# Two products of each row pair first, and low parts by transfers, in a two-layer Fourier and attention encoder

## The chip, the cores and the metric

The kernel runs on one core of one Trainium2 chip. The metric is the device time of one execution in microseconds, the median of several. The core's engines run side by side, each with its own queue in program order: TensorE (PE, matrix products, with weight loads shown apart as PEld), VectorE (DVE), ScalarE (ACT), GpSimd (POOL) and SyncE (SP), which issues transfers. Products go into PSUM, which has eight banks here; everything else works in SBUF.

## The reference

Two layers on x, 512 positions by 1024 channels, float32:

```python
for l in range(DEPTH):
    h = rmsnorm(x, norm1[l])
    p = h @ w_in[l]                       # u (512) | q (8 x 64) | k (2 x 64) | v (2 x 64)
    y_f = fourier_mix(u, w_fourier[l], b_fourier[l])     # Re FFT over positions and channels, then @ w_f + b_f
    y_a = windowed_gqa(rope(rmsnorm(q)), rope(rmsnorm(k)), v, sink[l])   # |i - j| <= 128, learned sink
    x = x + concat(rmsnorm(y_f), rmsnorm(y_a)) @ w_o[l]
    h = rmsnorm(x, norm2[l])
    up = dwconv_centred(h @ w_up[l], conv_w[l], conv_b[l])   # 2 x 2816 columns, 3 taps along positions
    gate, val = up[..., :D_FF], up[..., D_FF:]
    x = x + (silu(gate) * val) @ w_down[l]
```

## The kernel before, in words

Everything is kept transposed: x is eight tiles of 128 channels by 512 positions (`x[0]` to `x[7]`). A matrix product in nearly full precision is done as three: each operand is split into a high part (a copy in the format float32r, written by ACT) and a low part (source minus high part, written by DVE), and `mm3` (L114) issues high by high, low by high and high by low. `split` (L98) does this for activations and `wsplit` (L132) for weights, into rotating buffers `whi` and `wlo`, five each. A `wsplit` reads a raw weight tile, `wraw` (three buffers of 128 x 1024), that `wload` (L127) brings through SP's queue.

**The feed-forward half of a layer** goes through the 22 blocks of 128 hidden channels in three groups of 8, 8 and 6 (`GROUPS`, L35; `kp` is half of that: 4, 4, 3). A group has two stages.

*Up projection* (L756 to L780). For each hidden block and each of gate and value: load 512 KB of `w_up`, two `wsplit`s, 24 matmuls into one PSUM bank; then DVE scales by the norm (`u`), ACT starts the convolution (`y`), DVE adds its other two taps. Silu and the product of gate and value give one block's activations. Two blocks make a pair, an upper and a lower one, from which `seven_gu` (L382) forms the right-hand operands of seven products: B11 from the upper block alone, the others (T1 to T4, B21, B22) from sums and differences of both blocks' halves. Their high and low parts go into parts of buffers that attention doesn't need at that time (`pieces`, L375; the names slab, pT and m4 in the profile).

*Down projection, the product stage* (L782 to L798). The output's 1024 channels are four pairs of tiles (`mp`), the 512 positions two halves, a group's hidden blocks two halves as well: a 2 x 2 by 2 x 2 block product that is done with seven products rather than eight. `seven_w` (L401) loads two tiles a and b of `w_down` (for the pair's two output tiles; the first half of each are the upper hidden blocks, the second half the lower ones: a11, a12, a21, a22) and yields, in this order, a weight, the bank part and the operand:

| product | weight | bank part | operand |
|---|---|---|---|
| 1 | a11 | X | B11 |
| 2 | s1 = a21 + a22 | Y | T1 |
| 3 | s2 = a11 - s1 | X | T2 |
| 4 | a12 | Z | B21 |
| 5 | s3 = a11 - a21 | X | T3 |
| 6 | s4 = a12 + s2 | Y | B22 |
| 7 | a22 | X | T4 |

The sums are DVE's, in buffers `tF` (six). X and Y share a PSUM bank and go on accumulating; after each product DVE adds the present content to a quarter of x. All seven of a row pair are done before the next pair's first. The banks are taken in turn from six (`FFN_BANKS`, L34). In layer 1's last group each quarter is sent out when its last term is in.

**Work done ahead for layer 1.** During layer 0's feed-forward half, `presplit` (L149) is a generator with 44 jobs, one for each tile of layer 1's weights, in the order qkv (16), u (8), f (4), o (16). A job loads a tile (`praw`, two buffers), folds it if it is u or f (DVE, into `tA`), splits it into two `tA` buffers (six in all) and stores both parts to DRAM (`kept`); the stores are called one job later. `fetch` (L193) loads the parts in layer 1. The loop calls `next(ahead)` once for every up projection and once at the first row pair of every product stage (L774, L784).

**What sets the order.** The program text gives each instruction a priority. A planner then simulates the program and puts on each engine's queue, at each moment, the earliest instruction in the text whose inputs and buffers are ready; a later one can so be put ahead of an earlier one that still waits. Buffers of one name are given out in the order of the text. On the chip each queue runs in the order so found. `tc.issue_after(ins)` ties the instructions of a block that are on the engine of `ins` behind `ins` in that queue, without waiting for it to finish.

Of the kernel before, what the change touches and what calls it, by code (L numbers as in the profile page):

```python
# [16 lines left out]
P = 128  # L17
D = 1024
S = 512
L = 2  # L20
# [17 lines left out]
def encoder_kernel(tc, t):  # L38
# [92 lines left out]

    def wsplit(raw, eng=None, hi_eng=None):  # L132
        hi = wp.tile([P, 512], F32R, tag="whi", name=nm("whi"), bufs=5)
        lo = wp.tile([P, 512], F32R, tag="wlo", name=nm("wlo"), bufs=5)
        n = raw.shape[-1]
        if hi_eng is None:
            act(hi[:, :n], raw)
        else:
            hi_eng.tensor_copy(hi[:, :n], raw)
        tt(lo[:, :n], raw, f(hi)[:, :n], ALU.subtract, eng)  # L140
        return hi, lo
# [7 lines left out]
    def presplit(l):  # L149

        late = []

        def keep(key, src):
            n = src.shape[-1]
            two = [temp(n, "tA", F32R) for _ in range(2)]
            split(two[0], two[1], src)
            kept[key] = [dp.tile([P, n], F32, tag=f"{key}{s}", name=nm("kept")) for s in range(2)]
            store()
            late.append(lambda: [nc.sync.dma_start(o, f(z)) for o, z in zip(kept[key], two)])

        def store():
            while late:
                late.pop()()

        def load(src):
            raw = temp(512, "praw")[:, :src.shape[-1]]
            nc.sync.dma_start(raw, src)
            return raw

        jobs = []  # L170
        for grp in (1, 0):
            for k in range(KT):
                c = (k % 2) * 384
                jobs.append((f"qkv{grp}{k}", lambda g=grp, k=k, c=c: load(t["w_qkv"][l, g, k // 2, :, c:c + 384])))
        for k in range(KT):
            jobs.append((f"u{k}", lambda k=k: load(t["w_in"][l, k * P:(k + 1) * P, 0:FW])))
        for j in range(NF):
            jobs.append((f"f{j}", lambda j=j: load_wf(l, j, temp(512, "praw"))))
        for half in range(2):
            for m in range(KT):  # L180
                jobs.append((f"o{half}{m}", lambda h=half, m=m: load(t["w_o"][l, h, :, m * 512:(m + 1) * 512])))
        got = jobs[0][1]()
        for n, (key, _) in enumerate(jobs):
            raw = got
            if n + 1 < len(jobs):
                got = jobs[n + 1][1]()
            keep(key, fold_wu(raw) if key[0] == "u" else fold_wf(raw) if key[0] == "f" else raw)
            yield
        store()
        while True:  # L190
            yield
# [181 lines left out]
    LANDED = {3: (0, 0), 4: (1, 1), 5: (0, 1), 6: (1, 0)}  # L373
# [27 lines left out]
    def seven_w(l, m, f0, kp):  # L401

        n = kp * P
        a, b = [wload(t["w_down"][l, m + i, :, f0 * P:f0 * P + 2 * n], 2 * n) for i in range(2)]
        a11, a12, a21, a22 = a[:, :n], a[:, n:], b[:, :n], b[:, n:]
        yield "X", wsplit(a11), "B11", 0, 0
        s1 = temp(n, "tF")
        tt(s1, a21, a22, ALU.add)
        yield "Y", wsplit(s1), "T1", 1, 1
        s2 = temp(n, "tF")  # L410
        tt(s2, a11, s1, ALU.subtract)
        yield "X", wsplit(s2), "T2", 0, 1
        yield "Z", wsplit(a12), "B21", 0, 0
        s3 = temp(n, "tF")
        tt(s3, a11, a21, ALU.subtract)
        yield "X", wsplit(s3), "T3", 1, 1
        s4 = temp(n, "tF")
        tt(s4, a12, s2, ALU.add)
        yield "Y", wsplit(s4), "B22", 0, 1
        yield "X", wsplit(a22), "T4", 1, 0  # L420
# [4 lines left out]
    for l in range(L):  # L425
# [326 lines left out]
        for f0, nf in GROUPS:  # L752
# [3 lines left out]
            for n in range(nf):  # L756
                fi = f0 + n // 2 + kp * (n % 2)
                ys_ = []
                for z in range(2):
# [10 lines left out]
                    act(y, u, AF.Identity, scale=cw[:, l, 1, m:m + 1], bias=cb[:, l, m:m + 1])  # L770
# [3 lines left out]
                    next(ahead)  # L774
# [6 lines left out]
            nxt = []  # L781
            for mp in range(KT // 2):  # L782
                if mp == 0:
                    next(ahead)  # L784
                xy, zz = [psum(FFN_BANKS[(nps[0] + i) % len(FFN_BANKS)]) for i in (1, 2)]
                nps[0] += 2
                bank = dict(X=xy[:, :256], Y=xy[:, 256:], Z=zz[:, :256])
                for i, (b, w, g, r, c) in enumerate(seven_w(l, 2 * mp, f0, kp)):
                    m, q0 = 2 * mp + r, 256 * c
                    for k in range(kp):  # L790
                        mm3(bank[b], [z[:, k * P:(k + 1) * P] for z in w], gu[k][g], k == 0 and i in (0, 3), k == kp - 1,
                            skip_group_check=True)
                    tt(x[m][:, q0:q0 + 256], x[m][:, q0:q0 + 256], bank[b], ALU.add)
                    if l == L - 1 and f0 + nf == FT and i in LANDED:
                        m, q0 = 2 * mp + LANDED[i][0], 256 * LANDED[i][1]
                        nc.sync.dma_start(t["out"][m, :, q0:q0 + 256], x[m][:, q0:q0 + 256])
                if l < L - 1 and f0 + nf == FT:
# [90 lines left out]
```

## Time and profile before

| | us |
|---|---|
| median of 3 runs | 1156.58 (1156.01 to 1157.02) |
| the profiled execution | 1156.34 |
| its span, first to last instruction | 1154.5 |
| PE busy | 1052.4 (91%) |
| DVE busy | 903.7 (78%) |
| ACT busy | 561.6 (49%) |
| POOL busy | 63.2 (5%) |

The profile is one execution. Lines such as L93 or L120 are lines of helpers (`tt`, `mm3`), so that instructions are told apart by the tiles that they write and read: `wlo<-wraw,whi` is a low part of a weight, `x<-x,ps` an addition of a product to x, `m<-tF,m`, `pT<-tF,pT` and `slab<-tF,slab` low parts of activations. An entry in square brackets is idle time of the engine ahead of the instruction, and what ended it. The granted clock (PEclk) is that of TensorE, as a share of full speed. Durations of neighbouring DVE or PE instructions overlap a little, so that their rate is read from their starts.

### The profile page before, as it was taken

How to read it: one execution, taken by the hardware profiler on the slowest of the kernel's cores; microseconds unless marked ns; L12 is line 12 of the kernel's file. 1: busy time of each engine (PE TensorE's matmuls, PEld its weight loads, DVE VectorE, ACT ScalarE, POOL GpSimd, SP SyncE). 2: the span in 40 equal slices, each digit the busy share in tenths (PEclk: the TensorE clock that was granted, in tenths of full speed). 3: DMA queues.
4: the chain of work that ended last, by engine and by line, in shares of the span. 5: the costliest groups of instructions: out<-in, count | busy, mean ns of one | idle time of the engine just before them, and what ended most of it. 6: DMA issues, size and time to landing. Idle time of an engine off the chain costs nothing.

```text
span 1154.5 us, 16570 instructions
## 1 busy us (share of the span) xinstructions
PE 1052.4 (91%) x5866; PEld 913.0 (79%) x5866; DVE 903.7 (78%) x1841; ACT 561.6 (49%) x1055; POOL 63.2 (5%) x142
## 2 busy tenths in 40 slices
PE   8999998993699996999789999999979999799977
PEld 8977786882688886988679977888869888698867
DVE  7967759888877878778785877378988688886876
ACT  5269636565334543344442596246543454334532
POOL 0015200001000000000000044000000000000000
PEclk9999999997799998999899999999989999899989
DMA  8231387887133221332146622423313422133213
GB/s 274 82 110 30 110 273 252 291 286 268 55 110 110 92 73 55 110 110 78 41 137 207 195 74 74 128 92 91 100 46 93 127 91 92 54 95 113 91 43 100
DMA packets 61559, 140.18 MB, mean 121 GB/s; under 512 B 6818, under 2 KB 22178, under 8 KB 61476
## 3 DMA queue, kind: packets, MB, share of 16 engines
q1 hardware_dynamic: 61476, 139.12, 38.5%
q8 instruction: 46, 0.75, 0.3%
q14 instruction: 37, 0.30, 0.1%
HBM read 116.02 MB, written 23.07 MB: 120 GB/s over the span
## 4 chain that ended last, share of the span: by engine, by line
PE 68%; DVE 16%; DMA 9%; ACT 4%; issue 2%; POOL 0%; SPq 0%; DVEq 0%; ACTq 0%; POOLq 0%
PE ps L120 20%; PE ps L121 20%; PE ps L122 20%; DVE tF L93 5%; DMA wraw<-in_w_down_dram 4%; DVE wlo L93 4%; PE ps L118 3%; DMA praw<-in_w_o_dram 2%; DVE x L93 2%; DVE tF L96 1%; DMA praw<-in_w_qkv_dram 1%; PE ps L595 1%; ACT tA L90 1%; DVE tA L93 1%; PE ps L588 1%
## 5 line engine op out<-in xcount | busy, mean ns | idle before, releaser
L120 PE MATMUL ps<-act,whi 128*128 128x512 f32 x768 | 299.2, 390 | 3.1 <-ACT whi L90 1.4
L122 PE MATMUL ps<-act,whi 128*128 128x512 f32 x768 | 298.5, 390 | 0.6 <-DVE act L96 0.5
L121 PE MATMUL ps<-act,wlo 128*128 128x512 f32 x768 | 298.4, 390 | 0.0
L90 ACT ACTIVATE whi<-wraw 128x512 fp32r<-128x512 f32 (+1 forms) x272 | 166.6, 616 | 220.3 <-PE ps L122 211.2
L93 DVE TENSOR_TENSOR wlo<-wraw,whi 128x512 fp32r<-128x512 f32 (+1 forms) x280 | 186.1, 669 | 37.9 <-ACT whi L90 35.9
L120 PEld LDWEIGHTS ps<-act,whi 128*128 128x128 f32 x768 | 144.2, 188 | 34.6 <-ACT act L90 2.1
L122 PEld LDWEIGHTS ps<-act,whi 128*128 128x128 f32 x768 | 144.2, 188 | 30.8 <-DVE act L96 1.4
L121 PEld LDWEIGHTS ps<-act,wlo 128*128 128x128 f32 x768 | 144.2, 188 | 29.6 <-DVE wlo L93 0.3
L96 DVE SCALAR_TENSOR_TENSOR tF<-tF,pb,tF 128x511 f32<-128x511 f32 x176 | 130.1, 747 | 13.5 <-ACT tF L90 11.4
L120 PE MATMUL ps<-slab,whi 128*128 128x256 f32 (+2 forms) x272 | 90.2, 336 | 33.5 <-ACT whi L90 27.7
L93 DVE TENSOR_TENSOR x<-x,ps 128x256 f32<-128x256 f32 (+1 forms) x184 | 81.0, 441 | 46.9 <-PE ps L122 42.1
L121 PE MATMUL ps<-slab,wlo 128*128 128x256 f32 (+2 forms) x272 | 88.6, 326 | 27.6 <-DVE wlo L93 27.4
L93 DVE TENSOR_TENSOR tF<-ps,rb 128x512 f32<-128x512 f32 x104 | 70.9, 687 | 44.6 <-PE ps L122 34.5
L90 ACT ACTIVATE whi<-tF 128x512 fp32r<-128x512 f32 (+1 forms) x96 | 57.0, 594 | 90.5 <-PE ps L122 69.6
L120 PEld LDWEIGHTS ps<-slab,whi 128*128 128x128 f32 x272 | 53.5, 198 | 41.6 <-ACT whi L90 29.3
L122 PE MATMUL ps<-slab,whi 128*128 128x256 f32 (+2 forms) x272 | 85.9, 318 | 0.4 <-DVE slab L93 0.3
L90 ACT ACTIVATE tF<-tF,pb 128x512 f32<-128x512 f32 x88 | 70.9, 809 | 29.7 <-DVE tF L93 25.8
L120 PE MATMUL ps<-pT,whi 128*128 128x256 f32 x264 | 78.6, 298 | 5.8 <-ACT pT L90 5.8
L121 PEld LDWEIGHTS ps<-slab,wlo 128*128 128x128 f32 x272 | 53.9, 198 | 34.3 <-DVE wlo L93 32.0
L121 PE MATMUL ps<-pT,wlo 128*128 128x256 f32 x264 | 78.3, 297 | 0.0
L93 DVE TENSOR_TENSOR wlo<-tF,whi 128x512 fp32r<-128x512 f32 (+1 forms) x96 | 61.3, 643 | 8.4 <-ACT whi L90 6.8
L122 PE MATMUL ps<-pT,whi 128*128 128x256 f32 x216 | 63.6, 294 | 0.0
(183 smaller groups left out, 1863.8 us busy)
## 6 DMA issues: line engine op xcount, KB each, us to landing
wraw<-in_w_up_dram SPq DMA_DIRECT2D x88, 512.0 KB, 3.6
wraw<-in_w_down_dram SPq DMA_DIRECT2D x32, 512.0 KB, 3.6
kept<-tA SPq DMA_DIRECT2D x56, 256.0 KB, 4.4
whi<-kept SPq DMA_DIRECT2D x28, 256.0 KB, 3.0
wlo<-kept SPq DMA_DIRECT2D x28, 256.0 KB, 3.7
kept<-tA SPq DMA_DIRECT2D x32, 192.0 KB, 3.6
wraw<-in_w_down_dram SPq DMA_DIRECT2D x16, 384.0 KB, 3.1
wraw<-in_w_o_dram SPq DMA_DIRECT2D x8, 512.0 KB, 3.7
```

Source lines behind the costliest of these rows:

```text
L90: return nc.scalar.activation(out, in_, func, **kw)
L93: return (eng or nc.vector).tensor_tensor(out, a, b, op=op)
L96: return nc.vector.scalar_tensor_tensor(out=out, in0=a, scalar=s, in1=b, op0=op0, op1=op1)
L118: nc.tensor.matmul(out, a[0], b[0], start=start, stop=stop, **kw)
L120: nc.tensor.matmul(out, a[0], b[0], start=start, stop=False, **kw)
L121: nc.tensor.matmul(out, a[1], b[0], start=False, stop=False, **kw)
L122: nc.tensor.matmul(out, a[0], b[1], start=False, stop=stop, **kw)
L588: tr = nc.tensor.transpose(pp[:, j * P:(j + 1) * P], pr[:, j * P:(j + 1) * P], ident)
L595: pv = nc.tensor.matmul(py[64 * e:64 * e + 64, i0 * P:(i1 + 1) * P], vp[:, j, 64 * g:64 * g + 64], pT[:, half, e, b0:b0 + 2 * (i1 - i0) + ...
```

## The change

Three parts.

1. `seven_w` is split into `first_two` and `other_five`. A product stage now does B11 and T1 of all four row pairs first, with four banks held for X and Y, and then the other five products of each pair in turn, for which a Z bank is taken. a11 is loaded for two pairs at once (half a `wraw` tile each) and again by `other_five`, in tiles `left` (a11, a21) and `right` (a12, a22). s2 is written as s3 - a22.
2. s1 is no longer a sum of DVE: SP loads a21 into a `sq` buffer (two of them), and POOL issues a transfer that adds a22 to it on the way. In the same manner, for the jobs of qkv and o, ACT writes the high part and its negative, and a transfer from POOL adds the source in DRAM to the negative; that is the low part. Jobs of u and f keep DVE's subtraction.
3. The ACT writes of a job are tied with `issue_after` to `pace[0]`, the last convolution or weight split on ACT ahead of it in the text. `next(ahead)` is called for three of every four up projections, and at every row pair of a product stage.

```diff
     def wsplit(raw, eng=None, hi_eng=None):
...
-            act(hi[:, :n], raw)
+            pace[0] = act(hi[:, :n], raw).ins
...
-        def keep(key, src):
+        def keep(key, src, dram):
             n = src.shape[-1]
             two = [temp(n, "tA", F32R) for _ in range(2)]
-            split(two[0], two[1], src)
+            if dram is None:
+                with tc.issue_after(pace[0]) if pace[0] is not None else nullcontext():
+                    act(two[0], src)
+                tt(two[1], src, f(two[0]), ALU.subtract)
+            else:
+                with tc.issue_after(pace[0]) if pace[0] is not None else nullcontext():
+                    act(two[0], src)
+                    act(two[1], f(two[0]), scale=-1.0)
+                nc.gpsimd.dma_start(f(two[1]), dram, accum_op=ALU.add)
             kept[key] = [dp.tile([P, n], F32, tag=f"{key}{s}", name=nm("kept")) for s in range(2)]
             store()
...
+            if key[0] == "u":
+                keep(key, fold_wu(raw), None)
+            elif key[0] == "f":
+                keep(key, fold_wf(raw), None)
+            else:
+                keep(key, raw, src)
...
+    def wd(l, m, f0, kp, half):
+        return t["w_down"][l, m, :, (f0 + half * kp) * P:(f0 + (half + 1) * kp) * P]
+
+    two_m = [None]
+
+    def first_two(l, mp, f0, kp):
         n = kp * P
+        s1 = temp(n, "sq")
+        nc.sync.dma_start(s1, wd(l, 2 * mp + 1, f0, kp, 0))
+        nc.gpsimd.dma_start(s1, wd(l, 2 * mp + 1, f0, kp, 1), accum_op=ALU.add)
+        if mp % 2 == 0:
+            two_m[0] = wtile()
+            for i in range(2):
+                nc.sync.dma_start(two_m[0][:, i * 512:i * 512 + n], wd(l, 2 * mp + 2 * i, f0, kp, 0))
+        yield "X", wsplit(two_m[0][:, mp % 2 * 512:mp % 2 * 512 + n]), "B11", 0, 0, False
+        yield "Y", wsplit(s1), "T1", 1, 1, False
+
+    def other_five(l, mp, f0, kp):
+        n = kp * P
+        left, right = wtile(), wtile()
+        for i in range(2):
+            nc.sync.dma_start(left[:, i * n:(i + 1) * n], wd(l, 2 * mp + i, f0, kp, 0))
+        for i in (1, 0):
+            nc.sync.dma_start(right[:, i * n:(i + 1) * n], wd(l, 2 * mp + i, f0, kp, 1))
+        a11, a21, a12, a22 = left[:, :n], left[:, n:2 * n], right[:, :n], right[:, n:2 * n]
+        s2, s3, s4 = [temp(n, "tF") for _ in range(3)]
         tt(s3, a11, a21, ALU.subtract)
+        tt(s2, s3, a22, ALU.subtract)
+        yield "X", wsplit(s2), "T2", 0, 1, False
+        yield "Z", wsplit(a12), "B21", 0, 0, True
+        yield "X", wsplit(s3), "T3", 1, 1, True
         tt(s4, a12, s2, ALU.add)
+        yield "Y", wsplit(s4), "B22", 0, 1, True
+        yield "X", wsplit(a22), "T4", 1, 0, True
...
-                    act(y, u, AF.Identity, scale=cw[:, l, 1, m:m + 1], bias=cb[:, l, m:m + 1])
+                    pace[0] = act(y, u, AF.Identity, scale=cw[:, l, 1, m:m + 1], bias=cb[:, l, m:m + 1]).ins
...
-                    next(ahead)
+                    if (2 * n + z) % 4 < 3:
+                        next(ahead)
...
             for mp in range(KT // 2):
+                nps[0] += 1
+                xy = psum(FFN_BANKS[nps[0] % len(FFN_BANKS)])
+                banks.append(dict(X=xy[:, :256], Y=xy[:, 256:]))
+
+            def products(mp, ws):
+                for b, w, key, r, c, landed in ws:
+                    for k in range(kp):
+                        mm3(banks[mp][b], [z[:, k * P:(k + 1) * P] for z in w], gu[k][key], k == 0 and key in ("B11", "B21"),
+                            k == kp - 1, skip_group_check=True)
                     m, q0 = 2 * mp + r, 256 * c
+                    tt(x[m][:, q0:q0 + 256], x[m][:, q0:q0 + 256], banks[mp][b], ALU.add)
+                    if landed and l == L - 1 and f0 + nf == FT:
                         nc.sync.dma_start(t["out"][m, :, q0:q0 + 256], x[m][:, q0:q0 + 256])
+
+            for mp in range(KT // 2):
+                products(mp, first_two(l, mp, f0, kp))
+            for mp in range(KT // 2):
+                next(ahead)
+                nps[0] += 1
+                banks[mp]["Z"] = psum(FFN_BANKS[nps[0] % len(FFN_BANKS)])[:, :256]
+                products(mp, other_five(l, mp, f0, kp))
                 if l < L - 1 and f0 + nf == FT:
                     nxt += [norm_tile(m, g1[:, l + 1, :], acc) for m in (2 * mp, 2 * mp + 1)]
```

More of the change, by code (lines that the diff above doesn't have):

```diff
@@ L130, in wload @@
         return raw[:, :n]
+    pace = [None]
     def wsplit(raw, eng=None, hi_eng=None):
@@ L173, in presplit, with begin @@
                 c = (k % 2) * 384
-                jobs.append((f"qkv{grp}{k}", lambda g=grp, k=k, c=c: load(t["w_qkv"][l, g, k // 2, :, c:c + 384])))
+                jobs.append((f"qkv{grp}{k}", t["w_qkv"][l, grp, k // 2, :, c:c + 384]))
         for k in range(KT):
-            jobs.append((f"u{k}", lambda k=k: load(t["w_in"][l, k * P:(k + 1) * P, 0:FW])))
+            jobs.append((f"u{k}", t["w_in"][l, k * P:(k + 1) * P, 0:FW]))
         for j in range(NF):
-            jobs.append((f"f{j}", lambda j=j: load_wf(l, j, temp(512, "praw"))))
+            jobs.append((f"f{j}", j))
         for half in range(2):
             for m in range(KT):
-                jobs.append((f"o{half}{m}", lambda h=half, m=m: load(t["w_o"][l, h, :, m * 512:(m + 1) * 512])))
-        got = jobs[0][1]()
-        for n, (key, _) in enumerate(jobs):
+                jobs.append((f"o{half}{m}", t["w_o"][l, half, :, m * 512:(m + 1) * 512]))
+        def begin(key, src):
+            return load_wf(l, src, temp(512, "praw")) if key[0] == "f" else load(src)
+        got = begin(*jobs[0])
+        for n, (key, src) in enumerate(jobs):
             raw = got
             if n + 1 < len(jobs):
-                got = jobs[n + 1][1]()
-            keep(key, fold_wu(raw) if key[0] == "u" else fold_wf(raw) if key[0] == "f" else raw)
+                got = begin(*jobs[n + 1])
+            if key[0] == "u":
[4 more added lines that the diff above has]
+                keep(key, raw, src)
             yield
@@ L366, in load_wu @@
         return [raw[:, k * 512:(k + 1) * 512] for k in range(2)]
-    LANDED = {3: (0, 0), 4: (1, 1), 5: (0, 1), 6: (1, 0)}
     def pieces(kp):
@@ L781, in encoder_kernel @@
             nxt = []
+            banks = []
             for mp in range(KT // 2):
[L783 to L788, printed above, removed]
-                    m, q0 = 2 * mp + r, 256 * c
[L790 to L795, printed above, removed]
-                        nc.sync.dma_start(t["out"][m, :, q0:q0 + 256], x[m][:, q0:q0 + 256])
+                nps[0] += 1
[6 more added lines that the diff above has]
+                            k == kp - 1, skip_group_check=True)
+                    m, q0 = 2 * mp + r, 256 * c
+                    tt(x[m][:, q0:q0 + 256], x[m][:, q0:q0 + 256], banks[mp][b], ALU.add)
+                    if landed and l == L - 1 and f0 + nf == FT:
+                        nc.sync.dma_start(t["out"][m, :, q0:q0 + 256], x[m][:, q0:q0 + 256])
+            for mp in range(KT // 2):
[5 more added lines that the diff above has]
+                products(mp, other_five(l, mp, f0, kp))
                 if l < L - 1 and f0 + nf == FT:
```

16 lines of the change are left out of this document (removed).

## The prediction

> **What bounds the kernel now.** The page first: span, engines, granted clock in 40 slices.
>
> ```profile
> span 1154.5 us, 16570 instructions
> PE 1052.4 (91%) x5866; PEld 913.0 (79%) x5866; DVE 903.7 (78%) x1841; ACT 561.6 (49%) x1055; POOL 63.2 (5%) x142
> PEclk9999999997799998999899999999989999899989
> ```
>
> PE is the bound, and the clock dips where each product stage opens. So next the view of stretches, cut where a stage begins (columns: length, busy us and instructions of PE, weight load, DVE, ACT, POOL, then clock, DMA share, GB/s).
>
> ```profile
> 152.50:301.60 149.10, 119.64 (x531) 96.89 (x530) 129.55 (x242) 80.57 (x137) 5.85 (x8) 0.91 0.76 251
> 268.40:343.10 74.70, 43.95 (x314) 41.72 (x313) 63.50 (x115) 31.66 (x53) 3.44 (x6) 0.79 0.41 129
> 343.10:434.40 91.30, 91.30 (x422) 76.26 (x420) 69.66 (x114) 42.65 (x68) 0.00 (x0) 1.00 0.31 94
> 434.40:485.20 50.80, 39.28 (x295) 38.17 (x294) 42.53 (x78) 19.84 (x33) 0.00 (x0) 0.90 0.26 77
> 555.40:607.00 51.60, 40.23 (x274) 37.31 (x273) 44.18 (x93) 24.30 (x45) 0.00 (x0) 0.90 0.33 100
> 847.50:896.90 49.40, 40.54 (x305) 39.56 (x304) 43.27 (x80) 20.48 (x34) 0.00 (x0) 0.90 0.29 86
> 1106.40:1152.00 45.60, 34.01 (x246) 31.56 (x244) 37.13 (x81) 16.48 (x31) 0.00 (x0) 0.93 0.29 87
> 987.80:1010.00 22.20, 15.25 (x97) 14.28 (x96) 19.86 (x37) 9.58 (x16) 0.00 (x0) 0.77 0.24 68
> 1010.00:1037.40 27.40, 25.50 (x209) 25.07 (x209) 23.32 (x44) 10.74 (x18) 0.00 (x0) 1.00 0.32 99
> 986.70:992.90 6.20, 1.40 (x13) 1.19 (x11) 5.69 (x11) 2.60 (x4) 0.00 (x0) 0.86 0.00 0
> ```
>
> Up projections are dense (91.30 of 91.30). Time is lost in the product stages, and the same stage of layer 0's first group (74.70) takes far longer than layer 1's (49.40). PE's timeline shows both:
>
> ```profile
> 268.99 0.28 PE L122 MATMUL ps<-slab,whi 128*128 128x256 f32 x1
> 275.11 0.58 PE L120 MATMUL ps<-pT,whi 128*128 128x256 f32 x1 [5.84 <-ACT pT L90]
> 290.85 0.58 PE L120 MATMUL ps<-m,whi 128*128 128x256 f32 x1 [14.59 <-ACT m L90]
> ...
> 986.50 0.28 PE L120 MATMUL ps<-slab,whi 128*128 128x256 f32 x1
> 987.81 0.28 PE L122 MATMUL ps<-m,whi 128*128 128x256 f32 x1
> 992.90 0.58 PE L120 MATMUL ps<-slab,whi 128*128 128x256 f32 x1 [4.80 <-ACT whi L90]
> 995.52 0.58 PE L121 MATMUL ps<-slab,wlo 128*128 128x256 f32 x1 [2.04 <-DVE wlo L93]
> ```
>
> Twelve matmuls of the first product start 986.50 to 987.81: 0.12 us each, 1.44 a product. Then PE waits 4.80 for the second operand and 2.04 for its low part, with DVE at work for 5.69 of 6.20. In layer 0's first group the wait is for the last row's activations (5.84, 14.59). Why, the view of the tile tA shows (form, count; durations min/median/max; first and last start):
>
> ```profile
> L159 SPq DMA_DIRECT2D kept<-tA x88: 319/327/757, 133.4 to 286.0; - x88
> L90 ACT ACTIVATE tA<-praw x32: 518/574/633, 132.8 to 284.5; 128x384 fp32r<-128x384 f32 x16, 128x512 fp32r<-128x512 f32 x16
> L93 DVE TENSOR_TENSOR tA<-praw,tA x32: 550/620/693, 134.0 to 285.1; 128x384 fp32r<-128x384 f32 x16, 128x512 fp32r<-128x512 f32 x16
> L93 DVE TENSOR_TENSOR tA<-praw x24: 405/419/428, 181.3 to 228.8; 128x255 f32<-128x255 f32 x16, 128x256 f32<-128x256 f32 x8
> L93 DVE TENSOR_TENSOR tA<-tA,tA x12: 672/688/695, 186.2 to 233.7; 128x512 fp32r<-128x512 f32 x12
> L334 DVE COPY tA<-praw x8: 161/169/171, 181.2 to 209.2; 128x2 f32<-128x2 f32 x8
> ```
>
> All 44 jobs (88 stores, two each) run between 133.4 and 286.0 although the program spreads their calls over three groups: each was put where it could first start. The first group carries them all, DVE falls behind its convolutions and PE runs dry.
>
> **The change, part by part.** The sum is made against the profiled execution's 1156.34 us (span plus 1.8); the median of the three runs is 0.24 above it.
>
> (1) Pacing. A job's ACT write is queued behind a convolution's (or a split's) ACT write, so the 44 jobs follow their 45 calls: 16 in group 0 (qkv), 16 in group 1 (8 u, 4 f, 4 o), 13 in group 2 (12 o and the last stores). For qkv and o DVE's subtraction goes too: 32 x 0.62 = 20 us. Without backlog layer 0's stretch should be layer 1's: 74.7 - 49.4 = **25.3 gained**. In its place come 32 ACT writes of 0.57; ACT is busy 42.65 of 91.30 in an up projection, and twelve jobs add 12 x 0.57 = 7: cost nothing. In a product stage four jobs add 2 x 4 x 0.63 = 5 to ACT's 20 of 50; uncovered that would be up to 5 us.
>
> (2) What pacing piles on group 1 of layer 0. u and f jobs still use DVE: 24 x 0.42 + 8 x 0.17 + 12 x 0.69 = 20 us. Group 1 now takes 91.3 + 50.8 = 142.1 with DVE busy 69.66 + 42.53 = 112; with the jobs, less S1 (below), 130. The target without them is 142.1 - 7 = 135. If DVE is kept as busy as under the load of the first group (129.55 of 149.10, 87%) it takes 149, 14 too long; if all fits, nothing. I take the middle, **7 lost**.
>
> (3) The opening of a product stage. What there is to gain: 987.80 to 1010.00 has 97 matmuls, 97 x 0.12 = 11.6 of 22.2; the rest of the stage 209 x 0.12 = 25.1 of 27.4. Lost: 10.6 + 2.3 = 12.9. DVE's pace comes from starts in its timeline, S1's sum from the grouped view:
>
> ```profile
> 991.44 0.68 DVE L93 TENSOR_TENSOR tF<-wraw 128x512 f32<-128x512 f32 x1
> 992.04 0.68 DVE L93 TENSOR_TENSOR m<-tF,m 128x512 fp32r<-128x512 f32 x1
> 992.64 0.42 DVE L93 TENSOR_TENSOR tF<-tF,tF 128x256 f32<-128x256 f32 x1
> 992.98 0.68 DVE L93 TENSOR_TENSOR m<-tF,m 128x512 fp32r<-128x512 f32 x1
> ...
> L93 DVE TENSOR_TENSOR tF<-wraw 128x512 f32<-128x512 f32 x4 | 2.8, 690 | 0.8 <-DMA wraw<-in_w_down_dram 0.7
> ...
> L93 DVE TENSOR_TENSOR tF<-wraw 128x384 f32<-128x384 f32 x4 | 2.2, 557 | 1.7 <-DMA wraw<-in_w_down_dram 1.7
> ```
>
> A full-width operation follows the last after 0.60, a half after 0.34. Now PE can start B11 and T1 of all four row pairs: eight products, 8 x 1.44 = 11.5, 986.5 to 998.0. B11 reads only the even row's activations, so four products (5.8 us) need nothing of the late chain: they cover the 4.80. DVE from 991.44, when the chain ends: rest of the activations 3 x 0.60 + 2 x 0.34 = 2.5; five of the eight low parts (of five buffers the last up row holds two, so three are made earlier) 3.0; eight additions to x 2.7; then s3, s2 and T2's low part 1.8: 1001.4. PE waits 3.4. After it a pair costs DVE 8 x 0.60 + 5 x 0.34 = 6.5, PE 5 x 1.44 = 7.2: PE sets the pace. Loss 3.4 + 2.3 = 5.7, gain 7.2; I take 7, four stages: **28 gained**. Ends: only S1's four sums go (2.4), or all loss (12).
>
> In the 3-piece stages a product is 9 x 0.12 = 1.08 and a 384-wide operation 0.55: PE wants T2 after 8.6, DVE has it after 4.7 (986.7 to 991.44) + 2.5 + 5 x 0.55 + 2.7 + 3 x 0.55 = 14.3, 5.7 late, then needs 6.1 a pair against 5.4 (2.8 more); with 2.3 as above 10.8, where 45.6 - 28 x 1.08 = 15.4 is lost now: 4.5 gained in layer 1, 4 in layer 0 (norms of the next layer fill DVE there): **8.5 gained**. Ends: S1's 2.2 alone, or 13 with no loss but the 2.3.
>
> [...]
>
> (4) Transfers. Per pair the loads grow from two of 512 KB to seven of 256 KB: at most 3 MB more a group, on 77 to 94 GB/s, where 251 GB/s was sustained: nothing. SP has time for the issues: it holds three w_down tiles 20 us before the stage opens.
>
> ```profile
> 963.61 11.83 SPq L129 DMA_DIRECT2D wraw<-in_w_down_dram  x3
> ```
>
> The accumulating transfer from POOL is not in this trace. Nearest rows:
>
> ```profile
> wraw<-in_w_down_dram SPq DMA_DIRECT2D x32, 512.0 KB, 3.6
> kept<-tA SPq DMA_DIRECT2D x56, 256.0 KB, 4.4
> ```
>
> Such a transfer reads from two sides and writes one. I bound it by one load, 3.6, and by a load and a store in turn, 8.0, and take 6, between the two. S1 of the first two pairs has its own two buffers and is early. The third starts when the first is split, before PE ends the up projection: 3.6 + 6 = 9.6 after, about when T1 of the third pair is due: nothing. Queued behind it on POOL are only other such transfers. On SP the store of a low part waits for one, with loads behind it; the job buffers decide how long it may last. There are six, two a job, so a job may hold its pair for three calls, and a call comes with every row of 24 matmuls:
>
> ```profile
> 266.13 0.39 PE L122 MATMUL ps<-act,whi 128*128 128x512 f32 x1
> ...
> 268.17 0.39 PE L122 MATMUL ps<-act,whi 128*128 128x512 f32 x1
> ```
>
> Nine starts in 2.04, so 24 take 5.4 and three rows 16 us; a job needs two ACT writes, 1.2, the transfer, 6, and its store, 4.4: 11.6, so this wait costs nothing. The outputs of layer 1's last group go out after the same four of seven products as now, and the end of the kernel stays as it is.
>
> Sum: 25.3 - 7 + 28 + 8.5 = 54.8; 1156.34 - 54.8 = 1101.5 us.
>
> **Rivals.** (B) S1 comes late. For it: two buffers, two chained transfers; against: 6 us fits. At 8 or more PE stalls about 2 us each at the third and fourth T1: 4 x 6 stages = 24: 1125.5. [...]
>
> (C) DVE, not PE, sets the openings, as its 5.69 of 6.20 suggests: PE waits just as long, only later in the opening, at T2 instead of T1, and the clock stays at 0.77 there. The gain is S1's sums alone, 4 x 2.4 + 2 x 2.2 = 14 instead of 36.5: 1124. Against it: the count of (3), by which the first 11.5 us of PE work wait for few of DVE's operations.
>
> (D) The change does not do what it says: jobs still crowd the first group, since only ACT is held and folds are not. Then 25.3 and the 7 both fall away: 1101.5 + 18.3 = 1120. Against it: every job's stores need the held ACT write.
>
> (E) Slower. An accumulating transfer of L us holds job buffers: a job keeps its pair for L + 1.2 + 4.4, and where that is more than three rows' 16 us, each job costs a third of it instead of its row's 5.4, with ACT's convolutions queued behind the job's write. At L = 18: (23.6 / 3 - 5.4) x 32 = 79: 1180. It decides from L = 16 (1159). Nothing here is that slow.
>
> **How the numbers follow.** Forecast 0.58, its own range 1086 to 1117; B 0.12; C 0.15; D 0.05; E 0.07; 0.03 for gains that just cancel. Below 1084 would need nearly all losses gone; above 1134 E or the cancelling case. So 1084 to 1134. Within 0.2% (2.3 us) is what cannot be told from no change. Faster: forecast, B, C, D, 0.90; same 0.03; slower 0.07.
>
> **What would show it.** Right for (1): stores of kept spread to about 590; PE's gap at about 275 to 293 gone; the clock near 1.00 in openings; for (2): DVE above 85% busy in layer 0's group 1; for (3): T1's products of four pairs ahead of the first T2, PE gaps under 4 us; for (4): S1 landed before its split is due. Wrong: gaps of PE ended by S1's split that waits for a transfer (B); DVE full with PE idle through the openings (C); SP or ACT held by tA (E).

## The result, and the profile after

The changed kernel takes **1118.3 us** (median of four runs, 1115.2 to 1123.2) against 1156.8 for the kernel before on the same chip: a ratio of 0.966, 95% interval 0.962 to 0.971. The forecast was 1101.5 with a range of 1084 to 1134: the direction and the range hold, and 17 us of the gain are missing.

The page of the changed kernel (its profiled execution took 1123.2 us, the longest of the four):

```profile
span 1121.4 us, 16901 instructions
PE 1053.4 (94%) x5866; PEld 916.6 (82%) x5866; DVE 863.8 (77%) x1785; ACT 574.5 (51%) x1087; POOL 112.2 (10%) x198
PEclk9999999999899998999899999999999999999989
```

DVE has lost 40 us of work (903.7 before), POOL has gained 49. The view of stretches, cut where the stages begin in this kernel (columns as in the prediction):

```profile
263.60:319.00 55.40, 44.48 (x314) 41.69 (x313) 39.35 (x77) 21.87 (x38) 7.82 (x9) 0.91 0.74 202
319.00:408.90 89.90, 89.90 (x409) 74.86 (x409) 81.35 (x156) 48.67 (x80) 0.86 (x1) 1.00 0.62 194
408.90:463.10 54.20, 43.33 (x314) 41.78 (x313) 40.42 (x79) 24.11 (x40) 6.10 (x7) 0.91 0.74 207
826.00:872.00 46.00, 41.61 (x326) 40.31 (x325) 39.83 (x76) 19.20 (x31) 2.57 (x3) 0.96 0.54 141
```

Layer 0's first product stage went from 74.7 to 55.4 us, its clock from 0.79 to 0.91; layer 1's from 49.4 to 46.0, with one product more done before the next up projection begins (the 49.4 start 1.3 us after that stage's first product; from it, it is 50.5). But layer 0's second stage still takes 54.2, where DVE is busy for only 40.42 and PE for 43.33, while the same work in layer 1, without jobs, takes 46.0. So something other than an engine's load holds layer 0's stages. The view of the tile tA, and the view of waits, say where to look:

```profile
L170 SPq DMA_DIRECT2D kept<-tA x88: 319/327/706, 203.7 to 571.1; - x88
...
L167 POOL DMA_DIRECT2D tA<-in_w_o_dram x16: 862/862/1217, 421.6 to 566.2; - x16
```

```profile
SPq L170 <- DMA tA<-in_w_o_dram: 62.1, 15, 7.0
SPq L170 <- DMA tA<-in_w_qkv_dram: 47.7, 13, 7.4
...
DVE tF L93 <- DMA wraw<-in_w_down_dram: 28.5, 15, 6.7
ACT whi L90 <- DMA sq<-in_w_down_dram: 28.1, 9, 4.9
```

The stores of `kept` are spread to 571 (they ended at 286): the pacing works. But SP stands 62.1 + 47.7 = 110 us at stores of low parts whose transfer has not landed; DVE's waits for w_down sum to 28.5; and ACT waits 28.1 for S1. One such place, in the timeline of layer 0's third product stage:

```profile
542.63 0.86 POOL L167 DMA_DIRECT2D tA<-in_w_o_dram  x1 [4.78 <-DMA wraw<-in_w_down_dram]
549.14 0.86 POOL L167 DMA_DIRECT2D tA<-in_w_o_dram  x1 [5.64 <-ACT tA L90]
...
543.25 0.86 SPq L445 DMA_DIRECT2D wraw<-in_w_down_dram  x2
549.49 0.33 SPq L170 DMA_DIRECT2D kept<-tA  x1
549.98 0.33 SPq L443 DMA_DIRECT2D wraw<-in_w_down_dram  x1
550.36 0.45 SPq L170 DMA_DIRECT2D kept<-tA  x1
550.85 0.46 SPq L443 DMA_DIRECT2D wraw<-in_w_down_dram  x1
...
547.21 0.55 DVE L93 TENSOR_TENSOR tF<-wraw 128x384 f32<-128x384 f32 x1
...
558.38 0.56 DVE L93 TENSOR_TENSOR tF<-wraw 128x384 f32<-128x384 f32 x1 [6.67 <-DMA wraw<-in_w_down_dram]
...
559.46 0.58 PE L121 MATMUL ps<-slab,wlo 128*128 128x256 f32 x1 [6.65 <-DVE wlo L93]
```

POOL issues a job's transfer at 542.63. SP has nothing to do from 544.1, but next in its queue is the store of that low part (549.49); behind the store stand the next pair's w_down loads (549.98, 550.85). DVE can start s3 from them only 7.5 us after the second (558.38); they run beside the next job's transfer (POOL at 549.14) and a store. DVE has waited 6.67 us and PE 6.65. It is the longest gap of PE in the product stages of this kernel. Not all of it is the store's: by the semaphores in the trace the two loads go into the buffer of the previous pair's left tile, which DVE read until 547.76 (the row at 547.21). So the loads went out 2 to 3 us late, and the larger part of the gap is that the second took 7.5 us, where the median w_down load of this kernel takes 3.6.

### The profile page after: what moved, and what is told of

Read it like the earlier page. It is cut to its first block, busy times and chain, and to the rows that moved or that the text cites. A ratio compares the mean times of both kernels' runs of the same rounds, so it can differ in the third digit from the quotient of the medians.

```text
span 1121.4 us, 16901 instructions
## 1 busy us (share of the span) xinstructions
PE 1053.4 (94%) x5866; PEld 916.6 (82%) x5866; DVE 863.8 (77%) x1785; ACT 574.5 (51%) x1087; POOL 112.2 (10%) x198
## 4 chain that ended last, share of the span: by engine, by line
PE 66%; DVE 11%; DMA 10%; issue 9%; ACT 2%; POOL 1%; SPq 0%; POOLq 0%; ACTq 0%; DVEq 0%
PE ps L122 19%; PE ps L120 19%; PE ps L121 19%; DMA sq<-in_w_down_dram 4%; DMA wraw<-in_w_down_dram 3%; PE ps L118 3%; DVE tF L93 3%; DVE wlo L93 2%; PE ps L630 2%; PE ps L623 1%; DVE x L93 1%; PE ps L611 1%; DMA tA<-in_w_o_dram 1%; DVE tF L96 1%; ACT whi L90 1%
## 5 line engine op out<-in xcount | busy, mean ns | idle before, releaser
L93 DVE TENSOR_TENSOR wlo<-wraw,whi 128x512 fp32r<-128x512 f32 (+1 forms) x280 | 186.4, 670 | 52.6 <-ACT whi L90 50.9
L120 PEld LDWEIGHTS ps<-slab,whi 128*128 128x128 f32 x272 | 52.7, 198 | 35.9 <-ACT whi L90 13.0
L90 ACT ACTIVATE whi<-tF 128x512 fp32r<-128x512 f32 (+1 forms) x72 | 42.4, 593 | 73.3 <-PE ps L122 55.7
L431 POOL DMA_DIRECT2D sq<-in_w_down_dram x24 | 21.5, 918 | 521.8 <-DVE wlo L93 226.8
```

The lines of the kernel that those rows point to most:

```text
L90: return nc.scalar.activation(out, in_, func, **kw)
L93: return (eng or nc.vector).tensor_tensor(out, a, b, op=op)
L120: nc.tensor.matmul(out, a[0], b[0], start=start, stop=False, **kw)
L431: nc.gpsimd.dma_start(s1, wd(l, 2 * mp + 1, f0, kp, 1), accum_op=ALU.add)
```

## The experiments

No kernel here leaves out any of the computation. In the three theories named in the expectations, Q is queues (what stands behind a wait), V the amount of DVE's work, T the amount of traffic. Times are medians; ratios are to the kernel before, run in turn with them. The medians of the kernel before lie between 1156.6 and 1159.4 us over these measurements, and the changed kernel's own interval is about 5 us to either side, so that differences of a few us between rows are not known.

| kernel | us | ratio, 95% | S1 by | jobs' low parts by | jobs in |
|---|---|---|---|---|---|
| changed kernel | 1118.3 | 0.962 to 0.971 | transfer | transfer | both stages |
| pace_only (old order) | 1136.7 | 0.978 to 0.984 | DVE | DVE | as before, paced |
| order_only | 1115.6 | 0.962 to 0.965 | DVE | DVE | as before, unpaced |
| both_dve | 1100.9 | 0.947 to 0.953 | DVE | DVE | both |
| jobs_dve | 1107.3 | 0.954 to 0.958 | transfer | DVE | both |
| s1_dve | 1105.9 | 0.952 to 0.958 | DVE | transfer | both |
| jobs_in_up | 1105.0 | 0.954 to 0.959 | transfer | transfer | up projections |
| lo_held | 1104.7 | 0.951 to 0.957 | transfer | transfer | both, low part stored late |
| up_dve | 1103.1 | 0.950 to 0.954 | DVE | DVE | up projections |
| s1_up | 1103.0 | 0.951 to 0.954 | DVE | transfer | up projections |
| s1_up_late | 1101.9 | 0.949 to 0.954 | DVE | transfer | up projections |
| lo_late | 1114.8 | 0.961 to 0.966 | transfer | transfer | both |
| s1_late | 1104.4 | 0.952 to 0.956 | DVE | transfer | both |

Lengths of the product stages in the profiled executions, from a stage's first product to the next group's up projection (layer 0's third to its last product there), in us by PE's timeline:

| kernel | layer 0 | | | layer 1 | | |
|---|---|---|---|---|---|---|
| before | 74.8 | 53.3 | 44.4 | 50.5 | 50.8 | 46.0 |
| changed kernel | 55.4 | 54.3 | 47.6 | 46.2 | 46.3 | 44.8 |
| pace_only | 57.5 | 51.8 | 44.2 | 54.6 | 51.7 | 46.5 |
| order_only | 68.9 | 44.1 | 37.1 | 44.6 | 45.3 | 37.6 |
| both_dve | 50.9 | 49.8 | 38.9 | 47.2 | 48.2 | 38.4 |
| s1_dve | 47.9 | 49.5 | 44.9 | 47.7 | 46.3 | 38.4 |
| jobs_in_up | 50.0 | 52.7 | 39.4 | 45.7 | 46.5 | 40.2 |
| lo_held | 49.1 | 54.0 | 41.6 | 44.4 | 44.4 | 40.1 |

**One part alone: the pacing.** The kernel before, with only the jobs' ACT writes tied behind a convolution's or split's:

```diff
-            act(hi[:, :n], raw)
+            pace[0] = act(hi[:, :n], raw).ins
...
-            split(two[0], two[1], src)
+            with tc.issue_after(pace[0]) if pace[0] is not None else nullcontext():
+                act(two[0], src)
+            tt(two[1], src, f(two[0]), ALU.subtract)
```

> The kernel before, with only the pacing of part 1: a job's ACT write is tied behind the last convolution or split, its subtraction stays on DVE, the products keep their old order. The prediction's terms give 25 gained in layer 0's first group and 7 lost where u and f fall: about 1138 us. If pacing is worth less than thought (DVE, with all 44 subtractions, is then short of time in the later groups), 1145 or more. If the missing time of the full change lies in pacing itself and not in the transfers, layer 0's product stages of groups 1 and 2 should already be longer here than before (53.3 and 52.5 us).

1136.7 us: 20 to 23 less than before, by which of the medians of before (1156.8, 1159.4) one takes. Layer 0's second and third stages are not longer than before (table), so the missing time is not in pacing by itself. Its stretches:

```profile
263.60:321.10 57.50, 42.95 (x314) 41.25 (x313) 49.38 (x94) 22.66 (x37) 0.00 (x0) 0.85 0.39 119
410.90:462.70 51.80, 41.63 (x314) 40.59 (x313) 45.20 (x84) 22.45 (x36) 0.00 (x0) 0.90 0.38 122
822.50:877.10 54.60, 42.88 (x314) 41.77 (x313) 44.58 (x81) 20.67 (x33) 0.00 (x0) 0.87 0.26 77
```

The first stage begins 4.8 us sooner (263.6 for 268.4) and is 17.2 shorter (57.5 for 74.7). Layer 1's, in which no job runs, became longer (54.6 for 50.5): the edit moved the planner's order of DVE there as well.

**The transfers, one at a time and both.** In jobs_dve DVE makes the jobs' low parts:

```diff
-                keep(key, raw, src)
+                keep(key, raw, None)
```

In s1_dve it makes S1, and in both_dve both edits are made:

```diff
-        nc.gpsimd.dma_start(s1, wd(l, 2 * mp + 1, f0, kp, 1), accum_op=ALU.add)
...
+            two_m[1] = wtile()
+            for i in range(2):
+                nc.sync.dma_start(two_m[1][:, i * 512:i * 512 + n], wd(l, 2 * mp + 2 * i + 1, f0, kp, 1))
...
+        tt(s1, s1, two_m[1][:, mp % 2 * 512:mp % 2 * 512 + n], ALU.add)
```

> The changed kernel (1118 us), but the low parts of all 44 jobs are DVE's subtraction again; S1 still comes by transfer. Theory Q (queue heads: in layer 0 SP's store of a low part waits for the job's transfer with w_down loads behind it, and S1's transfer stands on POOL behind a job's that waits for ACT): layer 0's product stages fall from 55, 54 and 56 us to 47 to 50, the total to about 1103 to 1110, although DVE gets 20 us of work back. Rival V (DVE's amount of work sets the openings): 20 us more of DVE in layer 0 makes it 1120 to 1130. Rival T (traffic: transfers are slow since the DMA engines are busy at 0.74): only 8 of some 40 MB go, so the stages stay within 2 us of the changed kernel's, 1116 to 1122.

> The changed kernel, but S1 is summed by DVE again (a21 by SP into its buffer, a22 into half a weight tile); the jobs' low parts still come by transfer. Theory Q: S1's split no longer stands in ACT's and DVE's queues waiting for a transfer ahead of the late chain, so openings of all six stages get 2 to 4 us shorter, less 4 x 0.6 of DVE: total 1105 to 1114; layer 1's stages (46 us) are where it must show. Rival V: 2.4 us of DVE more in each of six stages makes it about 1130. Two more weight tiles per stage in three buffers could delay the loads of the other five products: then layer 1's stages get longer, not shorter.

> The changed kernel without any accumulating transfer: pacing and the new order of products only, S1 and all low parts by DVE. Theory Q: both holds are gone, 1098 to 1108, and layer 0's stages come within 4 us of layer 1's. Rival V: DVE has 20 us more in layer 0 and 14 us more in all stages: 1125 to 1145.

Each alone gives 11 and 12 us back, both 17.4: 1100.9, the forecast's number, and faster than both kernels. V falls: DVE has 27.6 us more work than in the changed kernel (891.4 for 863.8), and the time is less. (In jobs_dve layer 0's stages took 52, 49.5 and 42 us; the first is outside the 47 to 50 expected.)

```profile
span 1100.5 us, 16815 instructions
PE 1046.8 (95%) x5866; PEld 910.9 (83%) x5866; DVE 891.4 (81%) x1841; ACT 559.6 (51%) x1055; POOL 64.8 (6%) x142
```

That s1_dve would show its gain in layer 1's 8-block stages was wrong: they stayed (47.7 and 46.3 us for 46.2 and 46.3). It came in layer 0 (47.9, 49.5 and 44.9 for 55.4, 54.3 and 47.6), where S1's transfers share POOL's queue with the jobs', and in the last stage; but of the 6.4 us there, most are not S1's, since jobs_in_up and lo_held, with S1 by transfer, take 40.2 and 40.1 where the changed kernel's profiled execution has 44.8.

**The order alone.** both_dve without the pacing, the calls where the kernel before has them:

```diff
-                with tc.issue_after(pace[0]) if pace[0] is not None else nullcontext():
-                    act(two[0], src)
+                act(two[0], src)
...
-                    if (2 * n + z) % 4 < 3:
-                        next(ahead)
+                    next(ahead)
...
+            next(ahead)
             for mp in range(KT // 2):
-                next(ahead)
```

> The new order of the seven products alone: no accumulating transfers (S1 and the low parts by VectorE, as in both_dve), and the jobs not paced: the calls stand where they stand in the kernel before, and the planner may run the jobs' high parts ahead. It asks whether the pacing's 20 to 23 us (pace_only) and the order's 36 (both_dve against pace_only) add up. If they add: both_dve plus 20 to 23, so 1121 to 1124, with layer 0's first product stage near 72 us and the kept weights stored by about 290 us. If the new order by itself takes part of the backlog's harm (its first eight products need less of VectorE), less is lost: 1108 to 1118. If the order needs the pacing (the backlog now delays the split of S1 and of the first blocks too), more: 1126 to 1140.

1115.6, the second case: the order is worth 41 us alone and 36 behind the pacing; the pacing 15 behind the order, 20 to 23 alone. Some of the two gains is the same gain. Its three stretches of layer 0, and then those of both_dve:

```profile
273.30:342.20 68.90, 43.78 (x314) 41.32 (x313) 61.25 (x113) 31.26 (x52) 2.56 (x6) 0.80 0.55 185
432.10:476.20 44.10, 40.91 (x314) 40.25 (x313) 39.56 (x75) 18.86 (x31) 0.00 (x0) 0.92 0.43 134
544.20:581.30 37.10, 32.12 (x235) 30.04 (x233) 35.60 (x79) 20.54 (x38) 0.00 (x0) 0.95 0.38 116
```

```profile
263.80:314.70 50.90, 43.85 (x314) 41.44 (x313) 47.59 (x93) 22.80 (x39) 0.00 (x0) 0.90 0.65 207
404.50:454.40 49.90, 42.78 (x314) 41.02 (x313) 45.01 (x87) 22.07 (x38) 0.00 (x0) 0.93 0.64 212
522.40:561.40 39.00, 31.68 (x235) 28.84 (x233) 37.64 (x83) 22.47 (x42) 4.61 (x6) 1.00 0.57 178
```

Pacing takes 18 us off the first stage and puts 5.8 and 1.9 on the next two, to which the jobs go.

**Where the transfers hurt.** The changed kernel with its transfers, but no job in a product stage; and the same without transfers:

```diff
-                    if (2 * n + z) % 4 < 3:
-                        next(ahead)
+                    next(ahead)
...
+            if l < L - 1 and f0 + nf == FT:
+                next(ahead)
             for mp in range(KT // 2):
-                next(ahead)
```

> The changed kernel with its transfers, but the jobs of layer 1's early weights are taken one at every tile of the up projections and none in the product stages (the last group's stage keeps one call for the last stores). The read-outs so far put 17 us of harm on the accumulating transfers; jobs_dve and s1_dve each took 11 to 12 of it away. Theory Q (heads of in-order queues: the low part's store on SyncE's queue, and S1's transfer behind a job's on GpSimd's, delay the product stages): with no job in a product stage neither is left there, the S1 transfers go out alone, and the time is that of jobs_dve or a little above, 1104 to 1111; layer 0's first two product stages 52 and 50 us, where they are 55.4 and 54.3. Theory T (the traffic that an accumulating transfer makes is the cost, wherever it stands): the traffic is the same, so 1115 to 1120. If the up projections now lose what the product stages gain (VectorE was 90% busy in layer 0's second up projection, and three more jobs go there), the time is also near 1118, but the up projections of layer 0 are then longer than 89.9 us.

> both_dve (no accumulating transfer) with the jobs in the up projections alone, as in jobs_in_up. VectorE is 90 to 94% busy in layer 0's product stages of both_dve (45.01 of 49.9 us in the second), and 81 to 90% in the up projections. If VectorE's load in layer 0's product stages is what still keeps them at 50 us where layer 1's are at 47 to 48, they come to 46 to 48 and the time to 1094 to 1099. If the up projections take the load only by growing, the time is 1099 to 1106, and they are longer than 90 us. If what is left in these stages is the loads' lateness, nothing changes: 1099 to 1103.

1105.0, as Q had it (though the first two stages took 50.0 and 52.7 us where 52 and 50 were expected), and 1103.1, no change. So the transfers cost 17 us with jobs in the product stages and 2 without, which is no more than the medians of before differ by (1156.6 to 1159.4), and for DVE's subtractions the place of the jobs makes no difference (1100.9 and 1103.1). T as the whole cause falls: the same traffic is moved in jobs_in_up. As a part of it T stands, as lo_held shows below. In the 52.7 us ACT waits 13.0 for S1 (7.0 in the changed kernel), so a late S1 costs there even with no job called in the stage. The up projection of layer 0's second group stays dense with four jobs more.

**Which queue.** First the low part's store was called one job later:

```diff
-            late.append(lambda: [nc.sync.dma_start(o, f(z)) for o, z in zip(kept[key], two)])
+            for s in range(2):
+                late.append([1 + (s == 1 and dram is not None), kept[key][s], two[s]])
```

> The changed kernel, but a low part that was made by an accumulating transfer is stored two jobs after it was begun instead of one, so that the transfer has landed when SyncE comes to the store; the high part is stored as before, and GpSimd's order is unchanged. It splits theory Q in two. If SyncE held by the store is the harm (the w_down loads issued behind it come late), the time falls by most of the 11 us that jobs_dve gave: 1106 to 1112, and SyncE's waits for tA, 110 us in sum with the changed kernel, are near none. If the harm is S1's transfer standing behind a job's on GpSimd's queue, nothing changes: 1115 to 1120, with SyncE's waits for tA gone all the same. In between, both count.

1114.8, but SP's waits are still there:

```profile
SPq L177 <- DMA tA<-in_w_o_dram: 59.3, 16, 7.2
SPq L177 <- DMA tA<-in_w_qkv_dram: 45.0, 13, 6.6
```

The planner puts a store where it reckons that its data are ready, and SP's order stayed what it was but for a few places. This kernel, and s1_late with the same edit on s1_dve, tested nothing; the intervals of the two kernels overlap, so the 3.5 us are not known either.

> S1 by VectorE (as in s1_dve, 1105.9 us), the jobs' low parts by transfers in the product stages too, but stored two jobs later, as in lo_late. GpSimd's queue then holds no product's transfer, and SyncE doesn't wait for a job's. s1_dve is 5 us above both_dve (1100.9), which has no accumulating transfer. If SyncE held by the store is these 5 us: 1099 to 1102, with layer 0's last product stage down from 44.9 us to about 40. If they are the traffic of the jobs' transfers, which take raw weights a second time beside the w_down loads, nothing changes: 1104 to 1108. In the changed kernel, where S1's transfers stand behind the jobs', the later store alone gave 3.5 us.

1104.4 where s1_dve has 1105.9, with SP's waits for tA at 79 us for 83. Then a version that binds: the store comes three jobs later and is tied behind a load on SP's own queue.

```diff
-                late.append([1 + (s == 1 and dram is not None), kept[key][s], two[s]])
+                late.append([1 + 2 * (s == 1 and dram is not None), kept[key][s], two[s]])
...
-                    nc.sync.dma_start(job[1], f(job[2]))
+                    with tc.issue_after(last[0]):
+                        nc.sync.dma_start(job[1], f(job[2]))
...
+            last[0] = nc.sync.dma_start(right[:, i * n:(i + 1) * n], wd(l, 2 * mp + i, f0, kp, 1)).ins
```

> lo_late and s1_late did not do what they were made for: SyncE's order of stores and loads stayed as in the changed kernel, since the planner puts a store where it reckons its data ready, and SyncE still waited 104 us for the low parts' transfers (110 with the changed kernel). Here the low part's store comes three jobs later and is tied behind the w_down load traced last before it, so that in SyncE's order it stands behind the loads of one more pair of row tiles. GpSimd's order is the same. SyncE's waits for tA in sum should fall from 110 us to under 60. If SyncE held by the store is the greater part of the transfers' 17 us, the time is 1104 to 1111 against 1118 for the changed kernel; if S1's transfer behind a job's on GpSimd is, 1113 to 1120.

1104.7, the first of the two cases: 13.6 less than the changed kernel, with every transfer in place and POOL's order kept. Its span is 1101.1 us. SP's waits, and its first stage in layer 1:

```profile
SPq L180 <- DMA tA<-in_w_o_dram: 28.2, 9, 6.1
SPq L180 <- DMA tA<-in_w_qkv_dram: 22.0, 10, 3.7
...
DVE tF L93 <- DMA wraw<-in_w_down_dram: 14.4, 11, 3.6
...
ACT whi L90 <- DMA sq<-in_w_down_dram: 26.5, 8, 4.2
```

```profile
814.10:858.50 44.40, 41.18 (x326) 39.56 (x325) 39.74 (x76) 19.11 (x31) 2.58 (x3) 1.00 0.53 147
```

SP's waits for tA fell from 110 to 50 us and DVE's for w_down from 28.5 to 14.4, while ACT's for S1 stayed (28.1, 26.5). Layer 0's first stage fell from 55.4 to 49.1 us, its third from 47.6 to 41.6; the second stayed (54.3, 54.0). Of the 20.3 us between the two spans, 8.4 are in layer 1's stages (46.2, 46.3 and 44.8 to 44.4, 44.4 and 40.1), where no job runs and the orders of DVE, ACT, SP and POOL are the same in both kernels; so with single profiled executions a stage is known to 2 to 5 us, and SP's holding can account for no more than about the 12.6 in layer 0.

The second stage shows what else there is. There SP's wait for tA went from 21.7 us to none, but DVE waits as long for w_down (7.0 and 6.9 us), and the stage did not get shorter. The loads themselves were slower beside the accumulating transfers: the median w_down load of this stage takes 7.0 us to land in the changed kernel, 5.9 in lo_held, 4.6 and 4.5 in s1_dve and jobs_dve, 3.8 in jobs_in_up and 3.1 in both_dve. How much of the 17 us this makes was not tested by itself.

**Combinations**, for a faster version. s1_up is s1_dve with the calls of jobs_in_up:

```diff
-                    if (2 * n + z) % 4 < 3:
-                        next(ahead)
+                    next(ahead)
```

> S1 by VectorE, the jobs' low parts by transfers, the jobs in the up projections alone. No accumulating transfer is left in a product stage and none is S1's. If their harm is in the product stages alone, this is as both_dve or better, since VectorE is rid of 32 subtractions of 0.69 us in the up projections, where it is 81 to 90% busy: 1097 to 1102. If a job's transfer also harms the up projections (SyncE held ahead of the loads of w_up), 1103 to 1107, near jobs_in_up (1105.0) and up_dve (1103.1).

s1_up_late has the edit of lo_late as well:

```diff
+                late.append([1 + (s == 1 and dram is not None), kept[key][s], two[s]])
```

> s1_up with the low parts stored two jobs later: SyncE held by a store in the up projections is taken away too. Against s1_up: the same (within 2 us) if SyncE has slack there, 2 to 5 us less if not.

1103.0 and 1101.9. Neither beats both_dve, although DVE is rid of the jobs' subtractions. Against up_dve (1103.1), from which s1_up differs only in who makes the low parts, there is no difference: with the jobs in the up projections it doesn't matter who makes them.

What follows from the table: four different cuts, each alone (jobs by DVE, S1 by DVE, no job in a product stage, SP not held), give 11.1, 12.4, 13.3 and 13.6 of 17.4 us back, too near to each other to be ranked. Had they been separate costs, they would add up to 50. Three of them take away or lessen the same thing, a job's low part that SP waits for in a product stage, and had to overlap. The two transfers are different things, and yet jobs_dve and s1_dve give 23.5 together where both_dve gives 17.4, so in part they cost the same time. The queues show a link, at the opening of layer 0's first stage:

```profile
263.83 0.86 POOL L431 DMA_DIRECT2D sq<-in_w_down_dram  x1 [5.47 <-DMA sq<-in_w_down_dram]
264.36 1.22 POOL L167 DMA_DIRECT2D tA<-in_w_qkv_dram  x1
...
270.60 0.33 SPq L170 DMA_DIRECT2D kept<-tA  x1
```

S1's transfer (263.83) has waited for S1's first half, which SP loads. The job's transfer stands behind it, though ACT had made its input by 261.0; it goes out at 264.36, and SP stands at the store of that low part until 270.60, with loads of the product stage behind. Two more jobs' transfers of layer 0 stand so behind S1's for 2.7 and 4.6 us, and one of S1's behind a job's that waits for ACT, for about 4. That these links and the slow loads make up the overlap is argued from the queues and not shown by a run; and how the 4 to 6 us that each single cut leaves are shared among slow loads, S1's lateness and the planner's order stays open.

## Why the prediction was right, and where it was wrong

**(1) and (2), the pacing: 25.3 gained less 7 lost, 18.3 in all.** Measured 20 to 23 alone. The sum was right, the parts less so. The 25.3 are 24.2 if layer 1's stage is taken from its first product (50.5 and not 49.4). Of them the first stage gives 17.2, and 4.8 come ahead of it, in the up projection, which the term left out. The 7 lost behind it are there in the new order (5.8 + 1.9 = 7.7, order_only to both_dve), but not as (2) put them: the up projection did not grow. In the changed kernel it is dense at 89.90 with DVE busy for 81.35, 90%; it is the product stages that pay. In the old order group 1 lost nothing (51.8), and layer 1's stage lost 4.1, for which no step stood. Rival D falls with the stores' last start at 571.1.

**(3), the openings: 28 + 8.5 = 36.5 gained.** Measured 36 (pace_only to both_dve), 41 without the pacing. The stage that the step counted to lose 5.7 over its products loses 7.3 in the changed kernel (46.2 for 27 products of 1.44), 8.3 in both_dve, 5.5 in lo_held. T2's wait of 3.4 did not come: the longest gap of PE in layer 1's first opening is 1.49 (its row stands below), ended by ACT's high part of an activation. The 6-block stage was mis-sized on the safe side: a loss of 10.8 was forecast, in both_dve layer 1's takes 38.4, 8.2 over 28 x 1.08. Rival C, DVE setting the openings with a gain of 14, falls. That (1) to (3) come to the 1100.9 of both_dve is luck in part: both_dve lacks the relief of DVE that their terms counted (S1's sums and the 32 subtractions), and misses of either sign cancel.

**(4), the transfers: nothing. This is the step that failed; it cost 17.4 us** (changed kernel to both_dve). The duration was right for the medians: 6 was taken, and the view of transfers has the rows below (single ones took up to 9.2):

```profile
sq<-in_w_down_dram POOLq DMA_DIRECT2D x16, 256.0 KB, 5.0
tA<-in_w_o_dram POOLq DMA_DIRECT2D x16, 256.0 KB, 6.0
tA<-in_w_qkv_dram POOLq DMA_DIRECT2D x16, 192.0 KB, 5.6
...
sq<-in_w_down_dram POOLq DMA_DIRECT2D x8, 192.0 KB, 4.2
```

Two sentences were wrong. "On SP the store of a low part waits for one, with loads behind it; the job buffers decide how long it may last ... so this wait costs nothing": the buffers may well hold, by its estimate for 11.6 of 16 us, but the loads named in that sentence were then left out of account. The store comes up right behind the transfer's issue, SP stands for up to 7.4 us, and the w_down loads behind it had no 7 us to spare; that SP held three tiles 20 us ahead of a stage says nothing of the eight tiles that the other five products load within it. And "Queued behind it on POOL are only other such transfers", set down as a reason for no cost, was no such reason: S1 is such a transfer, and with the jobs in the product stages the two kinds stand behind each other, mostly the job's behind S1's. The traffic, put at nothing, was a third error: the 3 MB a group left out that a job's transfer reads its weight from DRAM once more, and the w_down loads of layer 0's second stage took 7.0 us beside the transfers and 3.1 without. Of its signs, "PE gaps under 4 us" (6.65) and "S1 landed before its split is due" (ACT waited 28.1) failed.

**Rivals B and E** had the two halves of this. B's mechanism is in the trace (ACT waits 28.1 us for S1), its price was 24 and S1 by DVE gives 12.4. E had SP held by tA, but from a transfer of 16 us on, by way of the job buffers; it came at 6 us, by way of the loads. Neither had the other in it, and alone neither is what the runs show. The time lies in the stated range because that reached up to such rivals; it is 1.3 us above the forecast's own.

## What to carry to other kernels

The price of a wait lay here not on the waiting instruction but on what was queued behind it (SP stood 110 us at stores of low parts in the changed kernel, and DVE waited 28.5 us for w_down loads; 50 and 14.4 in lo_held): for each wait that a change adds, list the next instructions on that in-order queue and how much slack each has, and look whether two queues come to wait for each other in turn. Taking 28 us of work off an engine that is not the bound gained nothing here and cost 17, through two queues and slower loads. When several single cuts each give back most of a loss, they take away the same time in part: don't add them up, and run the version with all of them.

## What the runs showed of the hardware

**The granted clock stood at 0.50 for a time in a stage where no wait of PE was longer than 1.49 us.** That is layer 1's first product stage of the changed kernel, from 844.0 to 847.4:

```profile
836.51 0.39 PE L120 MATMUL ps<-m,whi 128*128 128x256 f32 x1 [1.49 <-ACT m L90]
838.05 0.39 PE L120 MATMUL ps<-slab,whi 128*128 128x256 f32 x1 [0.57 <-DVE x L93]
840.52 0.38 PE L120 MATMUL ps<-slab,whi 128*128 128x256 f32 x1 [0.42 <-ACT whi L90]
841.39 0.39 PE L120 MATMUL ps<-slab,whi 128*128 128x256 f32 x1 [0.49 <-DVE x L93]
842.66 0.39 PE L121 MATMUL ps<-slab,wlo 128*128 128x256 f32 x1 [0.88 <-DVE wlo L93]
```

```profile
826.00:844.00 18.00, 14.16 (x110) 13.16 (x109) 15.05 (x30) 7.83 (x13) 2.57 (x3) 1.00 0.73 173
844.00:847.40 3.40, 2.91 (x15) 2.61 (x13) 3.40 (x7) 1.25 (x2) 0.00 (x0) 0.50 0.22 58
847.40:872.00 24.60, 24.54 (x204) 24.54 (x205) 21.38 (x41) 10.11 (x17) 0.00 (x0) 1.00 0.44 130
```

Five waits add up to 3.85 us between 835.0 and 842.7. In lo_held the same stage, without the 1.49, has a clock of 1.00 over its 44.40 us (the row under lo_held above):

```profile
824.95 0.39 PE L120 MATMUL ps<-slab,whi 128*128 128x256 f32 x1 [0.56 <-DVE x L93]
827.42 0.38 PE L120 MATMUL ps<-slab,whi 128*128 128x256 f32 x1 [0.42 <-ACT whi L90]
828.29 0.39 PE L120 MATMUL ps<-slab,whi 128*128 128x256 f32 x1 [0.49 <-DVE x L93]
829.56 0.38 PE L121 MATMUL ps<-slab,wlo 128*128 128x256 f32 x1 [0.88 <-DVE wlo L93]
```

There the waits add up to 2.35 us. But the 1.49 ended 7.5 us ahead of the stretch at 0.50, and that it decides is not shown; nor do the runs show what else does. Half of the 3.40 us at 0.50 gives 1.7 as an estimate of what this cost.

**A transfer that accumulates took 1.4 to 1.9 times as long as a plain one here.** The medians in the changed kernel's execution are 5.0 (S1) and 6.0 us (low parts) at 256 KB, where plain loads of the same size take 3.6 (w_down) and stores 3.2 (kept). The bounds of 3.6 and 8.0 that the prediction worked out from loads and stores held for the medians; single ones landed up to 9.2 us after their issue. Plain loads of w_down beside them were slower too (a median of 7.0 us in layer 0's second stage, 3.1 without them in both_dve).
